# A two-layer hybrid decoder step: the tile scheduler orders VectorE, ScalarE, GpSimd and DMA work with a timeline simulator

## The chip, the core and the metric

The kernel runs on one NeuronCore of one Trainium2 chip. The metric is the device time of one execution in microseconds (us), the median of several. The core's engines work in parallel, each through its own list of instructions from top to bottom: TensorE (PE in the profile, with its weight loads as PEld), VectorE (DVE), ScalarE (ACT), GpSimd (POOL), and SyncE (SP), which here only issues DMA. An instruction that waits for another engine holds up everything behind it in its own list.

## The reference, cut to what is computed

Two layers over 544 tokens (a prompt of 512, and 8 samples of 4), in float32, with a width of 1024:

```python
h = rmsnorm(x, p['norm1_g']) * (1 + mod[:, 1]) + mod[:, 0]
z = h @ p['w_in']          # pooling, retention, short conv, RWKV-7 and the merge gates
yA = pool_mixer(...); yB = retention(...); yC = short conv; yD = rwkv7_mixer(...)
proj = jnp.einsum('btnc,ncd->btnd', branches, p['w_br'])
gates = jax.nn.sigmoid(z[..., COL_GATE:].reshape(B, T, N_BRANCH, D_MODEL))
mixed = jnp.sum(gates * proj, axis=2) @ p['w_out']
x = x + mod[:, 2] * mixed
h2 = rmsnorm(x, p['norm2_g']) * (1 + mod[:, 4]) + mod[:, 3]
up, n_ffn = causal_dwconv(h2 @ p['w_up'], st_ffn, p['ffn_w'])
x = x + mod[:, 5] * ((jax.nn.silu(up[..., :D_FF]) * up[..., D_FF:]) @ p['w_down'])
```

`mod` is a linear map of silu(c), c being the condition of the prompt and of each sample. A last RMSNorm gives y; the new states of all branches are outputs too.

## The kernel before, in words

Activations lie with channels on the 128 partitions and tokens along the free axis, in two halves of 272 tokens (`HS`). Every large product is made in three passes: weights and activations are split into a rounded part (hi) and the rest (lo), and PE adds hi*hi, hi*lo and lo*hi into one PSUM tile (`mm3`, L133 to L135). A **unit** is one block of 128 output channels for one half: 8 blocks of K, so 24 matmuls, or 6 where K is 256. Its result is a `pd` tile. The pool of these (`psd`) has three buffers, so a unit can begin only when the tile three units back, or whichever held its buffer, has been read out.

For the weights `load_unit` issues a DMA into a `raw` tile (three buffers), ACT casts it to `whi` (L113), and DVE subtracts to get `wlo` (L114); `whi` and `wlo` have four buffers each. Activations are split the same way by `split_hilo` (L394 on ACT, L395 on DVE).

The steps of a layer, in PE's order, with the lines the prediction names:

- **Head** (first layer only): `ada_first(k)` makes the modulation of block k (L207 matmuls, L209 copy on ACT, L212 matmuls, L214 and L196 on DVE); L942 on DVE multiplies x by the norm's factor, L290 having made that factor; L297, L300, L301 modulate; `first_units(k)` starts the first six units, k by k.
- **Branches**: the RWKV scan has small matmuls that wait for short copies (L615 on DVE before L620, L481 before L500). `retention` ends with a norm (L388 and L391 on ACT, with loads of the activation table, L872 and L873 on DVE).
- **Gates** (once for each branch): long units whose tile ACT reads out with a sigmoid (L1129), and short `project` units of 6 matmuls, in fours, whose tiles DVE multiplies by the gate (L1111) and which L1113 adds up on GpSimd, or on DVE in the last gates. The last gates also split the sum with L394 and L395.
- **W_out** on that sum: `residual` reads the tile out (L346, and for the second half also L350 and L353), L276 and L279 sum the squares, L287 adds over partitions, L290 inverts, and `norm_half` makes the next input (L309, L297, L394, L395) while the next half's units run.
- **FFN**: units of W_up are read out by ACT (L1274), convolved (L1039 to L1041), and W_down follows, again through `residual`, into the next layer's norm.

Two mechanisms set the order of instructions. On PE it is the order of the code, under `manual_schedule`. On all other engines the scheduler of the tile framework orders the instructions, in the kernel before by its own estimates; a read-out in the code stands under `tc.high_priority()`:

```python
with tc.high_priority():
    V.tensor_tensor(out=a[:, c0:c1] if first else gs, in0=pp[:, :HALF], in1=gs, op=MUL)   # L1111
if not first:
    (V if last else G).tensor_tensor(out=a[:, c0:c1], in0=a[:, c0:c1], in1=gs, op=ADD)    # L1113
if last:
    split_hilo(a[:, c0:c1], mix[m // 4][:, m % 4, c0:c1], mix[2 + m // 4][:, m % 4, c0:c1])
```

## Time and profile before

| | |
|---|---|
| time, median of 3 runs | 1978.6 us (1977.38 to 1979.33) |
| the profiled execution | 1977.9 us, span 1976.1 us |
| PE busy | 1908.5 us, 97% |
| DVE, ACT, POOL busy | 1111.4 us, 831.2 us, 315.7 us |

The profile is that of one execution. Its span runs from the first to the last instruction, so 1.8 us of the execution's own time lie outside it. Busy time counts the instructions themselves. A row of the timeline ends with the idle time before it in square brackets, and with what ended that idle time; idle time on an engine matters only where PE ends up waiting for it.

### The profile page before, as it was taken

Reading aid. Unit: us, or ns where it says so; the run is one execution under the profiler, and the core shown is the slowest. Engines: PE = TensorE matmul, PEld = TensorE weight load, DVE = VectorE, ACT = ScalarE, POOL = GpSimd, SP = SyncE. Lnnn points to the kernel's source line nnn. Section 1 sums busy time; section 2 is a strip of 40 time slices with the busy share of each in tenths; the row PEclk is TensorE's granted clock in tenths of the full one; section 3 lists DMA queues with packets and bytes.
Section 4 is the critical chain, followed back from the end, with each engine's and each line's share of the span. In section 5 each row is a group of like instructions: output and inputs, shape, how many; then the busy total and the mean of one; then the engine's idle time right before and its main releaser. Section 6 shows DMA issues by size and latency. Waiting matters only on the chain.

```text
span 1976.1 us, 39220 instructions
## 1 busy us (share of the span) xinstructions
PE 1908.5 (97%) x16188; PEld 1829.6 (93%) x16188; DVE 1111.4 (56%) x2267; ACT 831.2 (42%) x1581; POOL 315.7 (16%) x627
## 2 busy tenths in 40 slices
PE   5999999999999999999999999999999999999997
PEld 4989888899999998899989899889999999999997
DVE  5466654643565653455673667556335765455565
ACT  4642332452445531435455433326424555243542
POOL 2120123213001210112201201232210012011210
PEclk8999999999999999999999999999999999999998
DMA  7323434423342257622332132124224222222231
GB/s 311 98 87 112 139 117 149 141 82 95 125 148 104 91 205 291 234 86 86 120 130 66 57 106 68 65 95 127 76 85 163 72 80 93 86 86 86 90 101 46
DMA packets 75555, 227.16 MB, mean 115 GB/s; under 512 B 20208, under 2 KB 23072, under 8 KB 73584
## 3 DMA queue, kind: packets, MB, share of 16 engines
q1 hardware_dynamic: 69872, 210.43, 31.9%
q0 software_dynamic: 3536, 11.53, 1.7%
q10 hardware_dynamic: 1968, 2.69, 0.5%
q8 instruction: 127, 2.08, 0.4%
q14 instruction: 52, 0.43, 0.1%
HBM read 213.33 MB, written 9.06 MB: 113 GB/s over the span
## 4 chain that ended last, share of the span: by engine, by line
PE 90%; DVE 5%; ACT 2%; DMA 1%; issue 1%; DVEq 0%; ACTq 0%
PE pd L133 27%; PE pd L135 26%; PE pd L134 26%; PE pm L236 2%; DVE wlo L114 1%; PE pm L673 1%; ACT whi L113 1%; DMA raw<-in_wst 1%; PE pm L500 1%; PE pm L677 1%; PE pm L653 0%; DMA t<-in_wada 0%; PE pm L507 0%; PE pm L620 0%; PE pm L383 0%
## 5 line engine op out<-in xcount | busy, mean ns | idle before, releaser
L133 PE MATMUL pd<-t,whi 128*128 128x272 f32 x4104 | 1207.3, 294 | 7.5 <-DVE zr L350 3.6
L135 PE MATMUL pd<-t,wlo 128*128 128x272 f32 x4104 | 1187.5, 289 | 0.0
L134 PE MATMUL pd<-t,whi 128*128 128x272 f32 x4104 | 1181.8, 288 | 0.1
L133 PEld LDWEIGHTS pd<-t,whi 128*128 128x128 f32 x4104 | 773.9, 189 | 39.9 <-issue 26.4
L134 PEld LDWEIGHTS pd<-t,whi 128*128 128x128 f32 x4104 | 775.7, 189 | 1.3 <-DVE t L395 0.3
L135 PEld LDWEIGHTS pd<-t,wlo 128*128 128x128 f32 x4104 | 774.3, 189 | 0.0
L114 DVE TENSOR_TENSOR wlo<-raw,whi 128x1024 fp32r<-128x1024 f32 x256 | 316.9, 1238 | 301.7 <-ACT whi L113 301.4
L113 ACT CAST whi<-raw 128x1024 fp32r<-128x1024 f32 x258 | 270.5, 1049 | 433.4 <-PE pd L134 419.6
L1276 POOL COPY off<-zr 128x18 f32<-128x18 f32 x88 | 76.2, 866 | 558.8 <-ACT zr L1274 558.8
L346 DVE SCALAR_TENSOR_TENSOR t<-pd,mod,t 128x272 f32<-128x272 f32 (+1 forms) x160 | 76.9, 481 | 112.5 <-PE pd L135 111.6
L1274 ACT COPY zr<-pd 128x272 f32<-128x272 f32 (+2 forms) x264 | 72.7, 311 | 78.4 <-PE pd L135 78.4
L1129 ACT ACTIVATE zr<-pd 128x272 f32<-128x272 f32 x128 | 50.3, 395 | 110.3 <-PE pd L135 106.2
L1111 DVE TENSOR_TENSOR zr<-pd,zr 128x272 f32<-128x272 f32 x96 | 41.1, 437 | 98.8 <-PE pd L135 98.1
L1113 POOL TENSOR_TENSOR t<-t,zr 128x272 f32<-128x272 f32 x64 | 71.3, 1133 | 112.5 <-DVE zr L1111 112.4
L1040 DVE SCALAR_TENSOR_TENSOR zr<-zr,par,zr 128x560 f32<-128x560 f32 x92 | 73.4, 800 | 10.0 <-ACT zr L1039 9.9
L1041 DVE SCALAR_TENSOR_TENSOR zr<-zr,par,zr 128x560 f32<-128x560 f32 x92 | 73.4, 801 | 2.8
L1039 ACT ACTIVATE zr<-zr,par 128x560 f32<-128x560 f32 x92 | 70.2, 765 | 6.8
L394 ACT CAST t<-zr 128x544 fp32r<-128x544 f32 (+1 forms) x96 | 49.5, 530 | 53.4 <-DVE zr L1287 53.0
L395 DVE TENSOR_TENSOR t<-zr,t 128x544 fp32r<-128x544 f32 (+1 forms) x96 | 54.5, 580 | 30.7 <-ACT t L394 30.4
L276 ACT ACTIVATE zr<-t 128x272 f32<-128x272 f32 (+1 forms) x72 | 32.2, 455 | 82.8 <-DVE t L346 54.6
L133 PE MATMUL pd<-t,t 128*128 128x272 f32 x224 | 64.8, 289 | 0.2
L134 PE MATMUL pd<-t,t 128*128 128x272 f32 x224 | 64.5, 288 | 0.0
(283 smaller groups left out, 1770.1 us busy)
## 6 DMA issues: line engine op xcount, KB each, us to landing
raw<-in_wst SPq DMA_DIRECT2D x276, 512.0 KB, 3.4
t<-in_wada SPq DMA_DIRECT2D x32, 1024.0 KB, 9.5
raw<-in_wada SPq DMA_DIRECT2D x24, 512.0 KB, 3.4
zr<-in_rope POOLq DMA_DIRECT2D x16, 272.0 KB, 3.6
t<-in_wada SPq DMA_DIRECT2D x8, 512.0 KB, 6.1
t<-in_xT SPq DMA_DIRECT2D x4, 544.0 KB, 6.1
zr<-zr ACTq DMA_DIRECT2D x32, 68.0 KB, 2.9
t<-in_xT SPq DMA_DIRECT2D x2, 1088.0 KB, 7.1
```

Of the source, the lines that this page charges most:

```text
L113: S.copy(hi, raw)
L114: (G if (l, u) in ((0, 1), (0, 2)) else V).tensor_tensor(out=lo, in0=raw, in1=hi, op=SUB)
L133: PE.matmul(ps, lhsT=a, rhs=xh, start=first, stop=False)
L134: PE.matmul(ps, lhsT=a, rhs=xl, start=False, stop=False)
L135: PE.matmul(ps, lhsT=b, rhs=xh, start=False, stop=last)
L346: V.scalar_tensor_tensor(out=x[:, c0:c0 + npc], in0=ps[:, :npc], scalar=gate[:, m, 0:1], in1=x[:, c0:c0 + npc], op0=MUL, op1=ADD)
L1039: S.activation(cv, u[:, 0:560], AF.Copy, scale=wcol(0))
L1040: V.scalar_tensor_tensor(out=cv, in0=u[:, 1:561], scalar=wcol(1), in1=cv, op0=MUL, op1=ADD)
L1041: V.scalar_tensor_tensor(out=cv, in0=u[:, 2:562], scalar=wcol(2), in1=cv, op0=MUL, op1=ADD)
L1113: (V if last else G).tensor_tensor(out=a[:, c0:c1], in0=a[:, c0:c1], in1=gs, op=ADD)
L1274: pad_evac(lambda o, i, sl: S.copy(o, i), u, ps, half, 2)
L1276: G.tensor_copy(off[:, 22 * s + j], u[:, 512:562].rearrange("p (x t) -> p x t", t=2)[:, 0:25:3, :])
```

## The change

One argument of the tile context. With it the scheduler uses a timeline simulator as its model of the machine when it decides in which order the instructions of DVE, ACT, POOL and the DMA queues stand. PE stays in the order of the code.

```diff
-    with tile.TileContext(nc) as tc:
+    with tile.TileContext(nc, schedule_with_timeline_sim=True) as tc:
         with tc.manual_schedule(engines={mybir.EngineType.PE}):
             tile_hybrid_step(tc, io)
```

The instructions stay the same but for four more loads of the activation table on ACT (two in each layer, between L388 and L391). PE's 14127 rows are the same. Taken as lists, the two DVE orders differ in 1483 lines, those of ACT in 681, of SP in 58 and of POOL in 34. Layer 2 repeats what layer 1 does. Three places in layer 1, all on DVE, follow; names are the program's, with their numbers.

**The last but one gates, their last four short units** (`pd_709` to `pd_712`; L872, L873 and L395 are the end of retention). Before:

```order
L872 TENSOR_TENSOR t4_670_4825<-t4_670_4825,zr_698_5016 128x544
L1111 TENSOR_TENSOR zr_678_4854<-pd_709_5090,zr_678_4854 128x272
L873 TENSOR_TENSOR t4_670_4825<-t4_670_4825,t4_614_4415 128x544
L1111 TENSOR_TENSOR zr_686_4910<-pd_710_5099,zr_686_4910 128x272
L114 TENSOR_TENSOR wlo_715_5129<-raw_713_5126,whi_714_5128 128x1024
L1111 TENSOR_TENSOR zr_696_4989<-pd_711_5108,zr_696_4989 128x272
L1111 TENSOR_TENSOR zr_701_5028<-pd_712_5117,zr_701_5028 128x272
L395 TENSOR_TENSOR t4_653_4663<-t4_670_4825,t4_653_4663 128x544
```

With the change:

```order
L872 TENSOR_TENSOR t4_670_4825<-t4_670_4825,zr_698_5016 128x544
L873 TENSOR_TENSOR t4_670_4825<-t4_670_4825,t4_614_4415 128x544
L395 TENSOR_TENSOR t4_653_4663<-t4_670_4825,t4_653_4663 128x544
L1111 TENSOR_TENSOR zr_678_4854<-pd_709_5090,zr_678_4854 128x272
L114 TENSOR_TENSOR wlo_715_5129<-raw_713_5126,whi_714_5128 128x1024
L1111 TENSOR_TENSOR zr_686_4910<-pd_710_5099,zr_686_4910 128x272
L1111 TENSOR_TENSOR zr_696_4989<-pd_711_5108,zr_696_4989 128x272
L1111 TENSOR_TENSOR zr_701_5028<-pd_712_5117,zr_701_5028 128x272
```

L873 and L395 now stand ahead of the first read-out L1111, and the subtraction of `wlo_715` ahead of the second. On ACT the read-out L1129 of `pd_705` has moved from before the loads of the table for L388 and L391 to behind them, and L394 of the same tile stands ahead of the cast `whi_714`.

**The end of the last gates and the start of W_out** (`pd_841` to `pd_844` are the last four short units; `pd_867` is the first unit of W_out; `zr_829` and `zr_838` are the first token half, which that unit reads, `zr_831` and `zr_840` the second). Before, from the first L395 of these four on:

```order
L395 TENSOR_TENSOR t4_766_5543<-t4_279_2273,t4_764_5541 128x272
L1113 TENSOR_TENSOR t4_279_2273<-t4_279_2273,zr_838_6139 128x272
L1113 TENSOR_TENSOR t4_279_2273<-t4_279_2273,zr_840_6166 128x272
L395 TENSOR_TENSOR t4_766_5543<-t4_279_2273,t4_764_5541 128x272 x2
L114 TENSOR_TENSOR wlo_853_6227<-raw_851_6224,whi_852_6226 128x1024
L346 SCALAR_TENSOR_TENSOR t4_845_6216<-pd_867_6258,mod_4_94,t4_845_6216 128x272
L395 TENSOR_TENSOR t4_766_5543<-t4_279_2273,t4_764_5541 128x272
L114 TENSOR_TENSOR wlo_856_6233<-raw_854_6230,whi_855_6232 128x1024
L114 TENSOR_TENSOR wol_862_6245<-raw_860_6242,woh_861_6244 128x1024
```

With the change, from the subtraction that has moved up furthest:

```order
L114 TENSOR_TENSOR wlo_853_6227<-raw_851_6224,whi_852_6226 128x1024
L1113 TENSOR_TENSOR t4_279_2273<-t4_279_2273,zr_829_6057 128x272
L1111 TENSOR_TENSOR zr_831_6084<-pd_842_6179,zr_831_6084 128x272
L1111 TENSOR_TENSOR zr_838_6139<-pd_843_6190,zr_838_6139 128x272
L1111 TENSOR_TENSOR zr_840_6166<-pd_844_6201,zr_840_6166 128x272
L1113 TENSOR_TENSOR t4_279_2273<-t4_279_2273,zr_831_6084 128x272
L395 TENSOR_TENSOR t4_766_5543<-t4_279_2273,t4_764_5541 128x272
L1113 TENSOR_TENSOR t4_279_2273<-t4_279_2273,zr_838_6139 128x272
L1113 TENSOR_TENSOR t4_279_2273<-t4_279_2273,zr_840_6166 128x272
L114 TENSOR_TENSOR wlo_856_6233<-raw_854_6230,whi_855_6232 128x1024
L114 TENSOR_TENSOR wol_862_6245<-raw_860_6242,woh_861_6244 128x1024
L395 TENSOR_TENSOR t4_766_5543<-t4_279_2273,t4_764_5541 128x272 x2
```

Three weight subtractions (`wlo_853`, `wlo_856`, `wol_862`) that stood behind the pair of L395 now stand ahead of it.

**The second half of W_out while the norm of the first half is made** (`pd_889` and `pd_896` are units of the second half, which L346 and then L350 read out). Before:

```order
L114 TENSOR_TENSOR wlo_912_6699<-raw_910_6696,whi_911_6698 128x1024
L346 SCALAR_TENSOR_TENSOR t4_845_6216<-pd_896_6582,mod_4_94,t4_845_6216 128x240
L395 TENSOR_TENSOR t4_849_6222<-zr_886_6519,t4_847_6220 128x272
L353 TENSOR_TENSOR t4_845_6216<-t4_845_6216,zr_887_6525 128x32
L114 TENSOR_TENSOR wlo_921_6769<-raw_919_6766,whi_920_6768 128x1024
L309 TENSOR_TENSOR zr_890_6537<-t4_845_6216,zr_885_6516 128x272
L309 TENSOR_TENSOR zr_891_6548<-t4_845_6216,zr_885_6516 128x272
L309 TENSOR_TENSOR zr_892_6559<-t4_845_6216,zr_885_6516 128x272
L346 SCALAR_TENSOR_TENSOR t4_845_6216<-pd_905_6635,mod_4_94,t4_845_6216 128x240
L309 TENSOR_TENSOR zr_893_6570<-t4_846_6217,zr_885_6516 128x272
L350 TENSOR_TENSOR zr_894_6576<-pd_889_6530,mod_4_94 128x32
```

With the change:

```order
L114 TENSOR_TENSOR wlo_912_6699<-raw_910_6696,whi_911_6698 128x1024
L353 TENSOR_TENSOR t4_845_6216<-t4_845_6216,zr_887_6525 128x32
L395 TENSOR_TENSOR t4_849_6222<-zr_886_6519,t4_847_6220 128x272
L346 SCALAR_TENSOR_TENSOR t4_845_6216<-pd_896_6582,mod_4_94,t4_845_6216 128x240
L309 TENSOR_TENSOR zr_890_6537<-t4_845_6216,zr_885_6516 128x272
L309 TENSOR_TENSOR zr_891_6548<-t4_845_6216,zr_885_6516 128x272
L309 TENSOR_TENSOR zr_892_6559<-t4_845_6216,zr_885_6516 128x272
L309 TENSOR_TENSOR zr_893_6570<-t4_846_6217,zr_885_6516 128x272
L350 TENSOR_TENSOR zr_894_6576<-pd_889_6530,mod_4_94 128x32
L114 TENSOR_TENSOR wlo_921_6769<-raw_919_6766,whi_920_6768 128x1024
```

L350, the last reader of `pd_889`, now stands ahead of the subtraction `wlo_921` instead of behind it. The same exchange occurs for the units that follow, and at the end of layer 1, where W_down's second half runs beside the norm of layer 2.

Elsewhere: in the head the DVE list has all sixteen L942 ahead of the subtraction `wlo_114` (before, ten of them), and the L214 of block 0 ahead of the last two; ACT has the copies L209 of blocks 0 and 1 ahead of the casts L113 they followed; SP issues the fifth block's condition weights (`in_wada0`) behind seven small loads, and the last three behind three loads of layer weights. In the RWKV scan four of the pooling branch's additions (L1156, L1157, L1172, L1173) stand ahead of the copies that PE's small matmuls wait for.

## Rows read from the trace of the kernel before

**Rows 1.** The page: the span, and busy time by engine.

```profile
span 1976.1 us, 39220 instructions
PE 1908.5 (97%) x16188; PEld 1829.6 (93%) x16188; DVE 1111.4 (56%) x2267; ACT 831.2 (42%) x1581; POOL 315.7 (16%) x627
```

**Rows 2.** Waits of PE: who waits for whom, total us, times, longest.

```profile
PE pm L620 <- DVE gs L615: 10.4, 10, 1.3
PE pm L212 <- ACT t L209: 9.0, 2, 5.5
PE pm L500 <- DVE zr L481: 8.4, 3, 4.0
PE pd L133 <- DVE zr L350: 8.2, 6, 2.8
...
PE pd L133 <- ACT zr L1274: 1.1, 1, 1.1
```

**Rows 3.** The page: groups by line (busy, mean ns, idle before).

```profile
L114 DVE TENSOR_TENSOR wlo<-raw,whi 128x1024 fp32r<-128x1024 f32 x256 | 316.9, 1238 | 301.7 <-ACT whi L113 301.4
```

**Rows 4.** Timeline, last but one gates of layer 1 (start, duration, engine, idle before).

```profile
433.95 0.66 ACT L391 ACTIVATE zr<-zr 128x544 f32<-128x544 f32 x1
...
435.28 0.43 DVE L1111 TENSOR_TENSOR zr<-pd,zr 128x272 f32<-128x272 f32 x1
435.63 0.72 DVE L873 TENSOR_TENSOR t<-t,t 128x544 f32<-128x544 f32 x1
435.77 0.39 PE L133 MATMUL pd<-t,whi 128*128 128x272 f32 x1 [1.25 <-DVE zr L1111]
...
437.15 0.64 ACT L394 CAST t<-t 128x544 fp32r<-128x544 f32 x1
```

**Rows 5.** Timeline, end of the last gates and start of W_out, layer 1.

```profile
535.97 0.44 DVE L1111 TENSOR_TENSOR zr<-pd,zr 128x272 f32<-128x272 f32 x1
...
538.23 1.05 ACT L113 CAST whi<-raw 128x1024 fp32r<-128x1024 f32 x1 [0.27 <-PE pd L134]
...
539.84 0.79 DVE L395 TENSOR_TENSOR t<-t,t 128x272 fp32r<-128x272 f32 x2
...
542.44 1.22 DVE L114 TENSOR_TENSOR wlo<-raw,whi 128x1024 fp32r<-128x1024 f32 x1
543.58 1.22 DVE L114 TENSOR_TENSOR wol<-raw,woh 128x1024 fp32r<-128x1024 f32 x1
```

**Rows 6.** Timeline, second half of W_out, layer 1.

```profile
572.91 1.23 DVE L114 TENSOR_TENSOR wlo<-raw,whi 128x1024 fp32r<-128x1024 f32 x1
...
576.17 0.36 PE L133 MATMUL pd<-t,woh 128*128 128x272 f32 x1 [1.21 <-DVE zr L350]
...
580.53 0.36 PE L133 MATMUL pd<-t,woh 128*128 128x272 f32 x1 [1.10 <-DVE zr L350]
```

**Rows 7.** Timeline, second half of W_down at the end of layer 1.

```profile
1015.17 0.37 PE L133 MATMUL pd<-t,whi 128*128 128x272 f32 x1 [2.82 <-DVE zr L350]
...
1022.59 0.19 DVE L350 TENSOR_TENSOR zr<-pd,mod 128x32 f32<-128x32 f32 x1
...
1023.22 0.29 PE L133 MATMUL pd<-t,t 128*128 128x272 f32 x1
...
1029.63 0.73 PE L287 MATMUL pm<-zr,cst 128*128 128x272 f32 x2 [0.67 <-DVE zr L279]
```

**Rows 8.** Timeline, the head.

```profile
17.70 3.54 DVE L942 TENSOR_TENSOR t<-t,zr 128x272 f32<-128x272 f32 x10
...
20.96 3.61 POOL L114 TENSOR_TENSOR wlo<-raw,whi 128x1024 fp32r<-128x1024 f32 x1 [6.24 <-ACT whi L113]
21.16 1.22 DVE L114 TENSOR_TENSOR wlo<-raw,whi 128x1024 fp32r<-128x1024 f32 x1
...
22.38 2.49 DVE L942 TENSOR_TENSOR t<-t,zr 128x272 f32<-128x272 f32 x1
...
30.85 0.60 PE L133 MATMUL pd<-t,whi 128*128 128x272 f32 x1
```

## The prediction

> **What bounds the kernel now.** The page comes first: PE is busy for 1908.5 of 1976.1 us [rows 1], so all that any order of the other engines can give back is the 67.6 us in which PE stands still. 1908.5 us over 16188 matmuls make 0.118 us for one, 0.7 us for a unit of 6 and 2.8 us for one of 24. PE's list does not change. An instruction that moves on another engine therefore counts only if it moves a moment at which PE is released, and a delay of PE at one place is carried to the end, since all that follows on the other engines depends on PE's results. The view of PE's waits names who releases it late: L212 in the head (9.0 us), the small copies of the RWKV branch (L620 10.4, L500 8.4), and L350 and L1274 as readers of a `pd` tile (8.2 and 1.1) [rows 2]. Third I went through the order place by place: for each read-out of a `pd` tile and each operand of PE that now stands behind something that ran later before, I compared what was put ahead of it with the slack that its reader had. Few places are left over; the others are hidden by the three `pd` buffers or by weights that are ready long ahead. The commonest thing put ahead is a weight subtraction, 1238 ns [rows 3]; DVE waits for its cast for 301.7 us in all, so it is free to be placed in many ways.
>
> **The change, place by place.** Ends below are made from the durations in the rows; DVE instructions in a row overlap a little (ten L942 take 3.54 us, 0.35 each [rows 8]), so a short one counts 0.35.
>
> Last but one gates. Before, `pd_711` waited 1.25 us for the first L1111, which ended at 435.71 [rows 4]. Now L873 and L395 stand ahead of it. L391 ends at 434.3 where it ended at 434.6, since a read-out has left the list ahead of it; L872 and L873, 0.72 each, run to 435.7, L394 (0.64), behind a table load and that read-out, to 436.5, L395 (0.7) to 437.2, L1111 to 437.6: PE starts at 437.6, not 435.8. Of the next unit of 24 the buffer now comes from the second L1111, behind the subtraction of 1.24: 437.6 + 1.2 + 0.4 = 439.2, where PE came to it after two units of 6 (435.8 + 2 x 0.9 with their start) at 437.6. That is +1.6 to +2.0; I take 1.8. Bounds 0.5 (the table load and L391 come earlier than I think) and 3 (L395 slowed by GpSimd). Twice: **+3.6**.
>
> Into W_out. `pd_867` begins when the last short unit ends, about 538.2 (the cast that waited for it began at 538.23 [rows 5]), and needs the L395 of `zr_838` for its 23rd matmul, 22 x 0.125 us later: 540.9. Before, that L395 ended at 540.63 [rows 5], just in time. Now: L1111 ends at 536.4, `wlo_853` at 537.5, eight short ones at 540.3, `wlo_856` and `wol_862` at 542.6 (they overlap to 1.14 each, as 542.44 and 543.58 show), and the two L395 (0.79) at 543.4. PE waits 2.4 us in the middle of a unit. The late L346 of this unit is harmless, since its buffer is wanted three units (8 us) later. Bounds 1.0 and 3.2. Twice: **+4.8**.
>
> Second half of W_out. PE waited 1.21 and 1.10 us for L350, which stood behind the subtraction of 572.91 and, at its next turn, behind five L395 and L279 [rows 6]. Now `wlo_921` and the L395 are behind it: L350 ends at 574.2 where PE's start at 576.17 shows 576.1, and the next at 577.4 where 580.53 shows 580.4, both ahead of PE. But what was passed is late next: the fourth L350 from there has three subtractions ahead of it, and by the same addition ends at 584.85 where PE would arrive at 584.1. So 2.31 gained and some given back: -2.0, bounds -2.3 and 0. Twice: **-4.0**.
>
> Start of W_up: the 1.05 us behind L1274 [rows 2] hang on L1041 of the first convolution pairs, which now stands ahead of an L395 of 0.7 us: **-1.0**, bounds -1.1 and 0; layer 2 had no such wait.
>
> End of layer 1. The same exchange: PE's 2.82 us [rows 7] fall to 0.6, since L350 has two subtractions fewer ahead of it. But of what was passed, three subtractions then stand together ahead of the L350 that releases the last unit of W_down, two of which ran behind it before. With 1.14 for each it is 2.1 later than the 1022.78 at which it ended, so 1024.9, and PE, which began that unit at 1023.22 [rows 7], begins it 1.7 later; the 0.67 us in front of L287 [rows 7] go. Net **+0.7** to +1.0, I take 0.7; bounds -2.8 and +2.5.
>
> Head. The copies L209 of blocks 0 and 1 no longer wait behind a cast, so the 9.0 us at L212 nearly go. That by itself gives nothing: the first units wait for block 0's modulated input, begun before at 30.85 [rows 8]. Now all sixteen L942 and a subtraction stand ahead of it. Two on GpSimd run meanwhile, and beside the first of these one L942 took 2.49 us instead of 0.35 [rows 8]. If both block DVE like that, L942 ends at 17.7 + 16 x 0.35 + 2 x 2.4 = 28.1, then subtraction, L214, L196, two L297 for each of two blocks, L394 (1.2 + 0.4 + 2.2 + 0.6): 32.5, or +1.7. If DVE passes GpSimd by, 4.3 earlier: -2.8. The rows show both: a subtraction on DVE took its usual 1.22 us from 21.16 on, inside GpSimd's 3.61 [rows 8]. I take **+1.5**, nearer to the blocked end, because it is an L942 that was blocked; upper bound +3. [...]
>
> Small things, each a fraction of a 1.24 us subtraction, an L1111 of 0.43 or a pooling addition ahead of a copy: L481 before L500 (+0.3 a layer), an L1113 ahead of an L1111 (+0.25), the pooling additions in the scan less three L620 waits that shorten by an L1111 (+0.4), the last L346 behind the final norm (+0.5 once): **+2.4**, bounds 0 and 6. The four table loads lie where ACT's read-outs have slack of two units, nothing; without that cover 1.3 us each.
>
> Sum: 3.6 + 4.8 - 4.0 - 1.0 + 0.7 + 1.5 + 2.4 = +8.0 us. The profiled execution took 1977.9 us itself, so 1985.9; it lies 0.7 below the median of the runs, so 1986.6 beside that. I forecast **1986**.
>
> **The rivals.** (a) The two places in the gates cost nothing, because the casts, and so the subtractions, come earlier than I place them. For it: raw weights are mostly there long before. Against it: `whi_855` waited for PE until 538.23 [rows 5], so `wlo_856` cannot come early. Without the W_out term: 1985.9 - 4.8 = 1981.1, no change; that is so from the point at which its 2.4 falls under 0.7. (b) GpSimd doesn't block the head: 1985.9 - 4.3 = 1981.6, no change. (c) All L350, L1274 and L212 waits go (18.3 us [rows 2]) and no later L350 pays: 1977.9 - 18.3 + 3.6 + 4.8 + 2.4 = 1970.4, faster; it decides once more than 14.8 of the 18.3 stay. Against it: at both places the passed subtractions meet a later L350. (d) More is lost in the head: ACT now has the first cast of the later layer weights ahead of block 2's L394; if that load lands late, each of block 2 and 3's inputs is late by some 3 us, and small losses reach their upper bound: 1985.9 + 3 + 3.6 = 1992.5.
>
> **How the numbers follow.** A measurement of this kernel can tell about 0.2%, 4 us, from no change. Chances: forecast 0.5; (a) 0.11, (b) 0.11; (c) 0.11; (d) 0.17. So faster 0.11, same 0.22, slower 0.67. The range leaves out most of (c) and a part of (d): 1974 to 1995; the forecast's own is 1982 to 1991.
>
> **What would show it.** In the changed profile: PE waits of about 2 us for L1111 in the last but one gates, and of about 2.4 us for L395 (by then a wait inside a unit) at W_out, in both layers; no L350 wait at the second half's start; L212 gone from the waits and the first unit of the head later than 30.85. I am wrong if the L395 wait isn't there, or if waits that I call gone come back elsewhere on L350.

## The result, and the profile of the changed kernel

The changed kernel takes 1993.6 us (median of four runs, 1989.6 to 1994.7) against 1979.0; the ratio is 1.0069, with a 95% interval of 1.0054 to 1.0084. It is slower by 14.7 us. The forecast was 1986 with a range of 1974 to 1995: the direction held, and the loss is almost twice the +8.0 of the sum. The time lies inside the range, but outside the forecast's own 1982 to 1991.

The page of the changed kernel, to stand beside [rows 1] (the profiled execution is its fastest, 1989.6 us):

```profile
span 1987.8 us, 39277 instructions
PE 1913.2 (96%) x16188; PEld 1833.9 (92%) x16188; DVE 1107.8 (56%) x2267; ACT 834.5 (42%) x1585; POOL 316.6 (16%) x627
```

The span is 11.7 us longer; the other 3 us of the 14.7 are that this execution lies 4.1 below the median of its kernel, and that of [rows 1] 1.1 below its own. The waits, to stand beside [rows 2]:

```profile
PE pm L500 <- DVE zr L481: 9.8, 4, 4.5
PE pm L620 <- DVE gs L615: 9.4, 10, 1.6
PE pd L133 <- ACT t L394: 8.5, 1, 8.5
PE pd L133 <- DVE zr L350: 5.5, 7, 2.2
PE pd L133 <- ACT zr L1129: 4.6, 2, 2.3
PE pd L134 <- DVE t L395: 3.5, 2, 1.8
PE pm L653 <- DVE z L691: 2.4, 2, 1.5
PE pd L133 <- DVE t L1111: 2.1, 3, 0.9
...
PE pm L212 <- ACT t L209: 1.0, 2, 0.5
```

L212 has fallen from 9.0 to 1.0 and L1274 is gone. New are L1129 (twice 2.3), L395 (1.8 and 1.7, with PE's L134 waiting, so in the middle of a unit), L691, and L394 in the head (8.5: the time of the L212 waits, spent at a later line).

Because PE's list is the same in both kernels, the start of each matmul can be set against its start before. The difference (the shift) is a staircase, and each step is what one place costs or gives: waits that grew or went, and also matmuls that run at half speed behind them in one of the two executions (at a granted clock of 0.50 a 128x272 matmul starts 0.227 us behind the one before it, at 1.00 0.125 us). The steps of 0.5 us and more:

| place | forecast, a layer | layer 1 | layer 2 |
|---|---|---|---|
| head, up to 57 us | +1.5 | +2.1 | |
| start of the scan, L500 | in "small" | +1.9 | 0 |
| rest of the scan: PSUM buffers, L653, L620, L742 | in "small" | +1.1 +1.0 +1.2 -0.9 +0.7 -1.2 | +0.7 +1.4 +0.6 -0.8 -0.9 +0.5 |
| matmuls at half speed in the scan, in the execution of before only | | -1.5 | -1.5 |
| last but one gates | +1.8 | +2.7 | +3.2 |
| an L1113 ahead of an L1111 | in "small" | +0.5 | +0.6 |
| into W_out | +2.4 | +2.4 | +3.0 |
| second half of W_out | -2.0 | -2.6 | -2.6 |
| start of W_up | -1.0 | -1.2 | |
| end of layer 1 | +0.7 | +1.9 | |
| end of layer 2 | in "small" | | +0.8 |

In the last but one gates the wait is there, but another releaser than forecast comes first. Timeline of the changed kernel:

```profile
434.90 1.28 ACT L388 ACT_TABLE_LOAD   x1
...
436.71 1.28 ACT L391 ACT_TABLE_LOAD   x1
438.00 0.66 ACT L391 ACTIVATE zr<-zr 128x544 f32<-128x544 f32 x1
438.68 1.28 ACT L1129 ACT_TABLE_LOAD   x1
439.97 0.40 ACT L1129 ACTIVATE zr<-pd 128x272 f32<-128x272 f32 x1
...
440.42 0.39 PE L133 MATMUL pd<-t,whi 128*128 128x272 f32 x1 [2.29 <-ACT zr L1129]
...
441.58 0.43 DVE L1111 TENSOR_TENSOR zr<-pd,zr 128x272 f32<-128x272 f32 x1
...
442.06 0.60 PE L133 MATMUL pd<-t,whi 128*128 128x272 f32 x1 [0.17 <-DVE zr L1111]
```

The L1129 that reads `pd_705` out stands behind three loads of the table of 1.28 us each, and `pd_710` needs the buffer of `pd_705`: PE waits 2.29 for it. When DVE's late L1111 comes to matter, PE is late already, and waits only 0.17 more for it at `pd_711` (0.62 in layer 2). But this L1111 still comes last. It ends at 442.0; less the 4.35 us by which PE was late on arrival that is 437.7, where the text has 437.6, and `pd_711` begins 1.9 us later than before in each layer, for the 1.8 forecast. The rest of the two steps, 0.7 and 1.3, is matmuls at half speed right behind. The granted clock is 0.59 from 440 to 444 us in layer 1, and 0.57 from 1420 to 1424 us in layer 2 (the row is the first of the two; its columns are named further down):

```profile
440.00:444.00 4.00, 3.41 (x14) 3.09 (x15) 2.90 (x6) 2.15 (x4) 1.91 (x2) 0.59 0.00 0
```

At W_out the rows are the forecast, some 7.3 us later (the pair of L395 ends at 550.65 where the text has 543.4): the two subtractions ahead of the pair of L395, and PE inside its unit:

```profile
547.59 1.22 DVE L114 TENSOR_TENSOR wlo<-raw,whi 128x1024 fp32r<-128x1024 f32 x1
548.73 1.22 DVE L114 TENSOR_TENSOR wol<-raw,woh 128x1024 fp32r<-128x1024 f32 x1
549.87 0.78 DVE L395 TENSOR_TENSOR t<-t,t 128x272 fp32r<-128x272 f32 x2
...
550.70 0.39 PE L134 MATMUL pd<-t,whi 128*128 128x272 f32 x1 [1.80 <-DVE t L395]
```

In the second half of W_out L350 stands ahead of the subtraction, the waits of 1.21 and 1.10 [rows 6] are gone, and one of 0.22 comes instead, further on:

```profile
584.03 0.18 DVE L350 TENSOR_TENSOR zr<-pd,mod 128x32 f32<-128x32 f32 x1
584.13 1.21 DVE L114 TENSOR_TENSOR wlo<-raw,whi 128x1024 fp32r<-128x1024 f32 x1
...
594.14 0.36 PE L133 MATMUL pd<-t,t 128*128 128x272 f32 x1 [0.22 <-DVE zr L350]
```

And at the end of layer 1 the wait of 2.82 [rows 7] has become four (0.41, 0.61, 1.72 and 2.18), the last of them behind two subtractions:

```profile
1018.46 0.36 PE L133 MATMUL pd<-t,whi 128*128 128x272 f32 x1 [0.41 <-DVE zr L350]
...
1025.78 0.36 PE L133 MATMUL pd<-t,t 128*128 128x272 f32 x1 [1.72 <-DVE zr L350]
...
1027.83 2.36 DVE L114 TENSOR_TENSOR t<-raw,t 128x1024 fp32r<-128x1024 f32 x2
1030.10 0.19 DVE L350 TENSOR_TENSOR zr<-pd,mod 128x32 f32<-128x32 f32 x1
...
1030.44 0.36 PE L133 MATMUL pd<-t,t 128*128 128x272 f32 x1 [2.18 <-DVE zr L350]
```

### The profile page after: what moved, and what is told of

Its sections match the earlier page's. It is cut to its first block, busy times and chain, and to the rows that moved or that the text cites. A ratio compares the mean times of both kernels' runs of the same rounds, so it can differ in the third digit from the quotient of the medians.

```text
span 1987.8 us, 39277 instructions
## 1 busy us (share of the span) xinstructions
PE 1913.2 (96%) x16188; PEld 1833.9 (92%) x16188; DVE 1107.8 (56%) x2267; ACT 834.5 (42%) x1585; POOL 316.6 (16%) x627
## 4 chain that ended last, share of the span: by engine, by line
PE 84%; DVE 8%; ACT 3%; issue 2%; DMA 2%; SPq 0%; DVEq 0%; ACTq 0%
PE pd L133 26%; PE pd L135 25%; PE pd L134 25%; PE pm L236 2%; DVE wlo L114 1%; PE pm L673 1%; DVE zr L290 1%; DMA raw<-in_wst 1%; PE pm L500 1%; PE pm L653 1%; ACT whi L113 1%; PE pm L507 0%; PE pm L677 0%; DVE t L942 0%; PE pm L620 0%
## 5 line engine op out<-in xcount | busy, mean ns | idle before, releaser
L134 PE MATMUL pd<-t,whi 128*128 128x272 f32 x4104 | 1182.0, 288 | 3.5 <-DVE t L395 3.5
L134 PEld LDWEIGHTS pd<-t,whi 128*128 128x128 f32 x4104 | 775.7, 189 | 5.2 <-DVE t L395 4.1
L113 ACT CAST whi<-raw 128x1024 fp32r<-128x1024 f32 x258 | 270.5, 1049 | 437.6 <-PE pd L134 427.4
L346 DVE SCALAR_TENSOR_TENSOR t<-pd,mod,t 128x272 f32<-128x272 f32 (+1 forms) x160 | 76.3, 479 | 115.9 <-PE pd L135 115.3
L1274 ACT COPY zr<-pd 128x272 f32<-128x272 f32 (+2 forms) x264 | 72.9, 311 | 85.2 <-PE pd L135 85.2
L1111 DVE TENSOR_TENSOR zr<-pd,zr 128x272 f32<-128x272 f32 x96 | 41.0, 436 | 102.7 <-PE pd L135 102.1
L1129 ACT ACTIVATE zr<-pd 128x272 f32<-128x272 f32 x128 | 50.6, 395 | 111.5 <-PE pd L135 103.1
L1113 POOL TENSOR_TENSOR t<-t,zr 128x272 f32<-128x272 f32 x64 | 68.6, 1088 | 121.0 <-DVE zr L1111 120.8
L1040 DVE SCALAR_TENSOR_TENSOR zr<-zr,par,zr 128x560 f32<-128x560 f32 x92 | 73.4, 801 | 7.1 <-ACT zr L1039 7.1
L395 DVE TENSOR_TENSOR t<-zr,t 128x544 fp32r<-128x544 f32 (+1 forms) x96 | 54.2, 578 | 31.8 <-ACT t L394 31.8
L394 ACT CAST t<-zr 128x544 fp32r<-128x544 f32 (+1 forms) x96 | 48.8, 531 | 47.9 <-DVE zr L1287 47.0
```

What stands on the lines that cost most here:

```text
L113: S.copy(hi, raw)
L134: PE.matmul(ps, lhsT=a, rhs=xl, start=False, stop=False)
L346: V.scalar_tensor_tensor(out=x[:, c0:c0 + npc], in0=ps[:, :npc], scalar=gate[:, m, 0:1], in1=x[:, c0:c0 + npc], op0=MUL, op1=ADD)
L1040: V.scalar_tensor_tensor(out=cv, in0=u[:, 1:561], scalar=wcol(1), in1=cv, op0=MUL, op1=ADD)
L1274: pad_evac(lambda o, i, sl: S.copy(o, i), u, ps, half, 2)
```

## The experiments

Most of the kernels are one of the two orders with pieces of the other. The instructions keep their places in the code; a function behind it draws an edge from each instruction of an engine to the next one that a table names, and the table is what an experiment changes:

```python
def pin_order(tc, nc):
    ins = nc.cur_bb.bb.instructions
    for at in ORDER.values():               # one list for VectorE, ScalarE, GpSimd, DMA queue
        for i, j in zip(at, at[1:]):
            tc.add_manual_dep(ins[j], ins[i].name, NoSync, reason="order")
```

Outside the places that an experiment names, the order of each engine's list in its trace is that of the kernel it starts from. Every ratio, and a difference with a sign, is against the kernel before as it ran beside that experiment (medians of 1979.0 to 1980.3).

**The two places in the gates, undone in the changed kernel, and alone in the kernel before.**

```diff
  VectorE, last but one gates (and so in layer 2)
- L872  L873  L395  L1111 pd_709  L114  L1111 pd_710 ...
+ L872  L1111 pd_709  L873  L1111 pd_710  L114 ... L395
  VectorE, end of the last gates
- L114 wlo_853  L1113 ...  L395  ...  L114 wlo_856  L114 wol_862  L395 x2
+ L1113 ...  L395 ... L395 x2  L114 wlo_853 ...  L114 wlo_856  L114 wol_862
  ScalarE, both places: the rows of before
```

> The changed kernel, with the order of before on VectorE and ScalarE at two places of each layer: the last four units of the last but one gates, and the end of the last gates with the start of W_out. Theory (each place counts by its own wait, added up to the end): the traces show +2.7 us and +2.4 us of shift there in each layer, so 1993.6 - 10.2 = 1983.4, and the waits of the first product of pd_710 for L1129 (2.3) and of L134 for L395 (1.8) are gone from the list. Rival 1 (a wait further on swallows what is saved, since something there does not follow PE): above 1988, with another wait longer by the same amount. Rival 2 (the loss is TensorE's clock after waits, not the waits): the waits go and the time falls by clearly more than 10, below 1981, because the matmuls behind the waits are shorter too.

Measured: 1983.7 us, ratio to before 1.0022 (1.0012 to 1.0032). The waits for L395 are gone, and those for L1129 fall from 4.6 to 1.0 us. So 10.0 us come back of the 11.1 that the steps in the table make, and nothing further on swallows much of them. This run and the next change VectorE's and ScalarE's lists together; no run parts the two.

> The kernel before, with the order of the changed kernel on VectorE and ScalarE at those two places of each layer and nowhere else. Theory: 1979.0 + 10.2 = 1989.2, with steps of 2.7 and 2.4 us in PE's start times against before at the two places of each layer. Rival 1: under 1984. Rival 2 (the clock after the waits): over 1991, with PE's busy time up by over 1.5 us. Rival 3 (the two places only hurt because the head or the scan had come late): no step at all, 1979.

Measured: 1994.8 us, 1.0075 (1.0063 to 1.0088). The steps are there (3.1 and 3.7 us in layer 1), so the first theory's places are right, but the whole is +15.4, not +10.2. PE is busy for 1917.5 us, 9.0 more than before: the second rival's sign. Counted from 100 us on, in the stretches with a granted clock of 0.50, the matmuls that follow one another at half speed lose 11.7 us in this execution, against 3.8 in that of before and 4.9 in that of the changed kernel. The largest piece, in the windows (columns: stretch, its length, busy time and count of PE, PEld, DVE, ACT and POOL, the granted clock, the DMA's share and GB/s), first of the kernel before and then of this one, at the second half of W_down in layer 1, where the two have the same order:

```profile
1012.00:1016.00 4.00, 1.18 (x9) 0.99 (x9) 4.00 (x11) 3.70 (x8) 0.00 (x0) 1.00 0.49 156
1016.00:1020.00 4.00, 3.25 (x26) 3.06 (x25) 3.81 (x13) 3.96 (x10) 0.00 (x0) 1.00 0.29 107
1020.00:1024.00 4.00, 4.00 (x33) 3.85 (x32) 3.78 (x11) 4.00 (x8) 0.00 (x0) 1.00 0.42 174
```

```profile
1016.00:1020.00 4.00, 1.60 (x13) 1.38 (x12) 4.00 (x8) 2.49 (x5) 0.00 (x0) 0.96 0.38 118
1020.00:1024.00 4.00, 3.59 (x16) 3.62 (x17) 2.83 (x10) 3.92 (x10) 0.00 (x0) 0.50 0.50 157
1024.00:1028.00 4.00, 3.25 (x15) 2.96 (x15) 2.88 (x10) 1.66 (x3) 0.00 (x0) 0.50 0.00 0
```

In its timeline the wait is the same as in [rows 7]:

```profile
1020.41 0.57 PE L133 MATMUL pd<-t,whi 128*128 128x272 f32 x1 [2.82 <-DVE zr L350]
```

Behind these 2.82 us the kernel before runs on at a granted clock of 1.00, 33 matmuls in 4 us; here the granted clock is 0.50, and 4 us hold 16. 33 matmuls at half speed cost 3.7 us here. Further such stretches, of 12 to 15 matmuls, stand behind the new waits of the gates in both layers and of W_out in layer 2, where before had none: 1.4, 1.7 and 1.7 us.

Such a stretch came without a long wait too. In the scan of the kernel before, PE is busy all the time from 330 to 334 us, 2 us of them with small matmuls (64x8, L704), and then loses 1.6 us in 14 matmuls at half speed; in the changed kernel the same small matmuls, from 337.2 us, are followed by a granted clock of 1.00 (337 to 345 us). The kernel before:

```profile
330.00:334.00 4.00, 4.00 (x95) 3.31 (x94) 2.95 (x6) 1.39 (x3) 3.05 (x4) 1.00 0.29 75
334.00:338.00 4.00, 4.00 (x21) 4.00 (x22) 1.33 (x3) 0.00 (x0) 1.64 (x4) 0.57 0.88 319
```

**The gains alone.** The kernel before, with the changed order only from the second half of W_out to the norm behind it, and at the start of W_up.

```diff
  VectorE, second half of W_out (and so in layer 2)
- L114 wlo_912  L346 pd_896  L395  L353  L114 wlo_921  L309 x3  L346 pd_905  L309  L350 pd_889
+ L114 wlo_912  L353  L395  L346 pd_896  L309 x4  L350 pd_889  L114 wlo_921
```

> The kernel before, with the order of the changed kernel only in the second half of W_out with the norm behind it (both layers) and at the first units of W_up (layer 1). Theory: the waits for L350 go and nothing comes back, -2.6 us in each layer and -1.2 once: 1979.0 - 6.4 = 1972.6. Rival 1 (what was passed is late at the units behind, so half is given back): 1975 to 1977. Rival 2 (the gain needs the late start that the gates made): 1979.

Measured: 1972.6 us (1972.1 to 1973.6), 0.9968 (0.9956 to 0.9980). Its steps are -2.7, -2.6 and -1.2, together -6.5. What was passed costs PE one wait of about 0.2 us in each layer.

**The rest alone.** The changed kernel, with both lists above put back to the order of before.

> The changed kernel with the order of before at all places of the two other lists (the gates, W_out and the first units of W_up), so that what is left of the change is the head, the scan, the end of layer 1 and the short exchanges. Theory by the sum on record: +0.7 (end of layer 1) +1.5 (head) +2.4 (small) = +4.6, so 1983.6. By the steps of the two traces it is 11.7 - 10.2 + 6.4 = +7.9, so 1986.9; then the terms of the head and the small places are too small by 3.3 in all, and the step at the start of the retention's scan (L500) and at two PSUM buffers of the scan shows it. Rival (these differ from execution to execution, since the time of after scattered by 5 us): within 1 us of before, with other steps than in the first trace.

Measured: 1988.3 us, 1.0045 (1.0033 to 1.0057). That is +8.9, so the remaining terms of the sum (4.6) are too small by 4.3. The next four kernels take them apart.

**The head alone, and the head without GpSimd.** The second one is not only an order:

```diff
-        (G if (l, u) in ((0, 1), (0, 2)) else V).tensor_tensor(out=lo, in0=raw, in1=hi, op=SUB)
+        V.tensor_tensor(out=lo, in0=raw, in1=hi, op=SUB)      # in VectorE's list behind the second L301
```

> The kernel before, with the order of the changed kernel only in the head (VectorE, ScalarE and the DMA queue, up to 75 us). Theory (the two GpSimd subtractions hold up L942 on VectorE): the waits at L212 go from 9.0 to about 1 us, two L942 take near 5 us together, the first unit starts about 1.2 us later than before, and the whole is +1.5 to +2.1: 1979.4 + 1.8 = 1981.2. Rival (the head catches up before the units of block 2 and 3, as the L212 waits are gone): within 0.5 of before from 60 us on.

Measured: 1982.4 us, 1.0016 (1.0007 to 1.0025), +3.4. The first unit starts 1.3 later, the shift is 2.2 at 57 us, and a further 1.8 comes at L500, at 118 us, where VectorE's and ScalarE's orders are those of before.

> As the run with the head alone, but the two subtractions of GpSimd in the head stand on VectorE instead, behind the second L301. Theory: without GpSimd beside them each L942 takes 0.35 us, so the sixteen end near 23.8 and not near 28, the first unit starts near 28.5 (32.0 in the changed kernel, 30.85 before), and the total falls by 3 us or so against the run with the head alone. Rival (the long L942 are not due to GpSimd, but to what else the moment holds, the DMA writes or the casts on ScalarE): two L942 still take 2 us or more each, and the first unit comes later by the 2.4 us of the two subtractions.

Measured: 1977.4 us, 0.9989 (0.9980 to 0.9998): 5.0 below the run with the head alone, and below the kernel before. The changed kernel's head first, then this one's:

```profile
18.02 4.95 DVE L942 TENSOR_TENSOR t<-t,zr 128x272 f32<-128x272 f32 x14
...
22.98 4.99 DVE L942 TENSOR_TENSOR t<-t,zr 128x272 f32<-128x272 f32 x2
...
21.60 6.06 POOL L114 TENSOR_TENSOR wlo<-raw,whi 128x1024 fp32r<-128x1024 f32 x2 [6.55 <-ACT whi L113]
...
32.06 0.59 PE L133 MATMUL pd<-t,whi 128*128 128x272 f32 x1 [8.54 <-ACT t L394]
```

```profile
18.04 4.95 DVE L942 TENSOR_TENSOR t<-t,zr 128x272 f32<-128x272 f32 x14
...
22.99 0.78 DVE L942 TENSOR_TENSOR t<-t,zr 128x272 f32<-128x272 f32 x2
...
27.87 0.60 PE L133 MATMUL pd<-t,whi 128*128 128x272 f32 x1 [4.87 <-ACT t L394]
```

Two L942 take 4.99 us beside GpSimd's subtractions and 0.78 without them. The fourteen ahead of them take 0.35 each, although GpSimd's first subtraction is already under way from 21.60. That subtraction, the last 1.38 us of the fourteen beside its start, takes 3.57 us, and the second 2.53.

**The scan alone, and the end of layer 1 alone.** The kernel before, with the changed order from 100 to 429 us and in the same part of layer 2; and from 1004 to 1062 us.

> The kernel before, with the order of the changed kernel only from the branches to the last but one gates (100 to 429 us, and the same part of layer 2). The sum on record has this at about +2.4 in all. Theory from the traces: the copies of the scan's start (L481) are late by 1.4 + 0.5, two units take another PSUM buffer and wait for a later reader (0.8 + 0.8), and L691 comes late (1.1), less 0.9 and a clock that falls elsewhere: +3 to +6, 1982.4 to 1985.4. Rival (the places of the scan are late only because the head is): 1979 to 1980, and no step at these units.

Measured: 1982.5 us, 1.0017 (1.0006 to 1.0028), +3.5. No step at L500 in layer 1: that one came with the head. Steps of 0.8 at `pd_300` (another PSUM buffer than before, waiting 0.8 for an L1111 that reads out `pd_295` in place of `pd_287`), 1.2 and 1.7 at L653 for L691, -0.9 and -0.8 at an L620.

> The kernel before, with the order of the changed kernel only at the end of layer 1 (1004 to 1062 us). Sum on record: +0.7. Theory from the traces: the wait of 2.8 falls to 0.5, two waits of 1.7 and 2.2 come three and four units later, L287 comes sooner: +1.3, and where the clock falls behind these waits up to 1.5 more: 1980.7 to 1982.2. Rival (the order gains as a whole once the first wait is gone): -1 or less.

Measured: 1979.6 us, 1.0004 (0.9995 to 1.0014): +0.65, not told from no change. The steps are -2.3, +1.6, +2.3 and -1.2. The head, the scan and the end of layer 1, each alone, make +7.6 of the +8.9 of the rest; the short exchanges that are left have no run of their own.

**The load of the table at L500.** In the changed kernel the buffer that the first L386 of layer 1 writes was last used by L1001 on GpSimd, and so L386 waits for GpSimd as well as for DVE. In its trace a semaphore instruction of L386 stands on ScalarE's queue at 106.0 us, and the load of the table comes right behind it, at 106.06, after a wait of 2.93. Before, L386 waited for DVE alone; the trace has no such instruction ahead of the first L386 (104.21), and the load came at 101.33, ahead of a wait of 1.59.

```diff
+        if floor is not None and not warmed: S.activation(warm, EPS6, AF.Ln, bias=ZERO); warmed.append(1)
         for c0, c1 in HS:       # the first of these logarithms is L386
```

> The changed kernel with one instruction more: a logarithm of a constant (128x1) on ScalarE ahead of the first L386 of layer 1, so that the load of the table stands ahead of L386's waits. Theory (the first L386 has a second semaphore to wait for, that of GpSimd, and the load of the table stands behind the first of the two waits, 1.28 us on the path of the scan's start): the step at L500 of the scan falls from 1.9 to about 0.6 us, and the total by 1.3, to 1992.3. Rival (L500 is late because of what stands ahead of L481 on VectorE, a subtraction of 1.24 and L1040): the load moves and L500 stays where it is, 1993.6.

Measured: 1991.8 us, 1.0057 (1.0045 to 1.0070). The total alone does not settle 1.3 us; the rows do. ScalarE in the changed kernel and in this one:

```profile
101.34 1.78 ACT L426 ACTIVATE t<-pm,par 128x272 f32<-128x272 f32 x4
106.06 1.28 ACT L386 ACT_TABLE_LOAD   x1 [2.93 <-DVE zr L385]
107.35 1.35 ACT L386 ACTIVATE zr<-zr,eps 128x272 f32<-128x272 f32 x3
```

```profile
101.75 1.79 ACT L426 ACTIVATE t<-pm,par 128x272 f32<-128x272 f32 x4
103.56 1.28 ACT L380 ACT_TABLE_LOAD   x1
104.86 0.29 ACT L380 ACTIVATE warm<-eps 128x1 f32<-128x1 f32 x1
106.51 1.44 ACT L386 ACTIVATE zr<-zr,eps 128x272 f32<-128x272 f32 x3 [1.36 <-DVE zr L385]
```

The load now lies in ScalarE's idle time, and the step at L500 is gone. PE's waits for L481 there, 4.88 us in the changed kernel (0.44 and 4.44), fall to 3.77, against 3.62 in the kernel before: 1.1 of the 1.9 us. The other 0.8 is matmuls of the scan at the lower clock: it stays at 0.50 until 126.7 us in the changed kernel, and is back at 1.00 by 124 in this one and by 123 in the kernel before. The subtraction and L1040 still stand ahead of L481 here, so the rival is out.

**The gates alone, without the wait at the end of layer 1.** The kernel with the gates alone, and the changed order from 1004 to 1024 us with three subtractions moved behind L350 and L346.

```diff
  VectorE, second half of W_down in layer 1, of the changed order
- L114 wlo_1473  ...  L350 pd_1494  L114 ...  L114 x2  L350 pd_1499  L346 pd_1505
+ ...  L350 pd_1494  L114 wlo_1473  L114 ...  L350 pd_1499  L346 pd_1505  L114 x2
```

> The run with the gates alone, and in it the order at the end of layer 1 in which TensorE no longer waits 2.8 us for L350 (nor later in that unit row). In that run's trace the gates' order cost 10.2 us by steps at its own places, and 4.0 us more by matmuls at the lower clock behind the wait of 2.8 us, at 1017 to 1030, where the order is that of before. Theory (the clock falls behind that wait): both go, 1994.8 - 3.0 - 4.0 = 1987.8, and no stretch of slow matmuls there. Rival (the slow stretch comes anyway, wherever the steps of the gates have moved it): 1991.8, with as many slow matmuls near 1017 to 1030 or later.

Measured: 1992.6 us, 1.0068 (1.0053 to 1.0083). The rival held. The wait of 2.82 is gone, but my order brought waits of 1.45, 1.04 and 2.56 for L350 at the units behind it, and behind the last of these, at 1034 to 1040 us, the granted clock is 0.72. So this run does not say what the clock costs when no wait is left there: the edit failed to take the cause away.

**Towards a better kernel.** First all that had gained, with that same order at the end of layer 1:

```diff
  kernel before: order of the second half of W_out and of the start of W_up as above
+ changed head, both GpSimd subtractions on VectorE, early load of the table
+ VectorE, last but one gates: L1111 x3  L872  L1111  L873  L114  L395
+ VectorE, one L620 of the scan, and the end of layer 1 as in the run above
```

> The kernel before with what the runs so far point to: the order of the changed kernel in the second half of W_out and at the start of W_up; its head, with the two subtractions of GpSimd on VectorE and the early load of the table; the order at one L620 of the scan; the first part of its end of layer 1, where L350 and L346 of two units stand ahead of two subtractions; and in the last but one gates the first three L1111 ahead of L872. Theory, place by place: -6.6 (second half, measured), -2.3 (head), -2.5 (1.25 at the gates, twice), -3.0 (end of layer 1), -0.9 (L620) = -15.3, so 1963.8. Rival (what is gained at one place is waited for at the next, or goes into a lower clock): above 1968.

Measured: 1968.6 us, 0.9946 (0.9933 to 0.9960): -11.7. The end of layer 1 lost (2.3 and 0.8 gained; 1.3, 1.2 and 2.5 given back), and in each gate PE now waits 1.2 for an L1129, which the old wait for L1111 had hidden.

> The best kernel so far without its order at the end of layer 1 (there the order of before stands again), and with one exchange on ScalarE in the last but one gates of each layer: the read-out L1129 of the last long unit ahead of a weight cast L113, since TensorE waited 1.22 us for it there. Theory: the end of layer 1 had given back 5.0 us after a gain of 2.0 and 0.75, so -2.3; the gates -1.0 in each layer: 1968.6 - 4.3 = 1964.3. Rival (the waits at the end of layer 1 were worth less than their steps, or the cast that now comes later is waited for at the next unit): 1967 or more, with a new wait for L114 or L113 behind the gates.

```diff
  ScalarE, last but one gates
- L391  L113 whi_714  L1129 pd_707  L394
+ L391  L1129 pd_707  L113 whi_714  L394
  end of layer 1: the order of before
```

Measured: 1966.7 us, 0.9936 (0.9923 to 0.9950), the lowest median of all and 26.9 below the changed kernel. It is 1.9 below the run before it, not 4.3, and since the intervals of the two overlap, neither of its two changes is shown to gain anything. PE still waits 1.03 for L1129 in each gate, one unit sooner, and behind the wait of 2.82 at the end of layer 1, which is back, 12 matmuls at half speed cost 1.4 us in this execution.

## Why the prediction was right, and where its sizes were off

**What bounds the kernel** held: the time moved where PE's release moved, and where its clock did. By the table's steps the sum of +8.0 has become +11.7: gates +2.3 more, W_out +0.6, second half -1.2, W_up -0.2, end of layer 1 +1.2, head +0.6, small things +0.4 (the remainder, with the steps under 0.5). The direction is that of the sum. The waits at the places that it names came out within 0.6 us a term, but for the second half with W_up; what it lacked is a term for the clock, and enough for the small things. That 1993.6 lies in the range is in part luck: it is outside the forecast's own 1982 to 1991, and the range reaches there for the sake of rival (d), which did not occur.

**Last but one gates.** +3.6 forecast, +5.9 by steps, of which 3.9 is the late release of `pd_711` and 2.0 matmuls at half speed. Place, sign and the queue on DVE hold, L1111's end to 0.1 us. The step that failed stands further down in the text: "The four table loads lie where ACT's read-outs have slack of two units, nothing". The units there are short ones of 0.9 us, and the L1129 of `pd_705`, behind L388's, L391's and its own load, is late by more than that: PE waits 2.29 for it. That costs little on top, since L1111 is later still.

**Into W_out.** +4.8 forecast, +5.4 by steps; place, releaser and mechanism are as written, and the subtractions did stand in the way. Rival (a) is out.

**Both gates together** are shown to be the largest loss: undone they give back 10.0 us, alone they cost 15.4. The sum had 8.4 and no term for the clock, which in the run with the gates alone made 7.9 of the loss.

**Second half of W_out and start of W_up.** -5.0 forecast, -6.4 by steps, -6.7 alone. Of the "some given back" little came: PE waits 0.2 us in each layer for an L350 there. This is the half of rival (c) that was true; its other half, that no later L350 pays, failed at the end of layer 1.

**End of layer 1.** +0.7 forecast, +0.65 alone, +1.9 in the changed kernel's trace, where 15 matmuls behind the wait of 2.18 run at half speed (1.7 us; the granted clock is 0.66 from 1030 to 1034 us). The mechanism is the one named, three subtractions together ahead of an L350.

**Head.** +1.5 forecast, +2.1 by 57 us, +3.4 alone. That GpSimd's subtractions hold up L942 is shown (two in 4.99 us beside them, in 0.78 without), and rival (b) is refuted with it. Why the L942 from 21.60 to 22.98 ran at 0.35 beside GpSimd is not shown. Missing was that a changed order also hands out buffers differently: L386 inherits one from GpSimd, and a load of the table comes onto the path at L500, 1.1 us of waiting by the run with the early load. Two slips in the text's addition: the 2.4 that each blocked L942 adds already holds its own 0.35, so 28.1 should be about 27.5 (measured 27.97), and 4.3 less than +1.7 is -2.6, not -2.8 (-3.0 measured without GpSimd). Rival (d) has the nearest number, 1992.5, but its mechanism did not occur: the inputs of blocks 2 and 3 are not 3 us late, the shift stays under 2.7.

**Small things.** +2.4 forecast within bounds of 0 and 6. They make +2.8 with L500, and the scan alone +3.5. But the 2.8 holds a gain that the order did not make: 3.0 us of matmuls at half speed in the scan that stood in the execution of before and not in this one. Without it they are +5.8, at the upper bound: this is the term that the sum had most wrong. Two kinds of place were not on the list, since no row that PE waits for is exchanged there: units that got another PSUM buffer, whose reader is a later one (waits of 0.86 and 0.81 in layer 1), and L691.

**Open** is what decides whether the clock falls. The wait of 2.82 us at the end of layer 1, with the same order in all of them, was followed by a granted clock of 1.00 in the profiled executions of the kernel before and of the second half alone, and by a lower one with the gates alone (0.50 from 1020 to 1028 us), with the head without GpSimd (0.50 from 1016 to 1020), and in the last kernel (0.70 from 1008 to 1012). Each kernel has the profile of one execution, so this may change from one execution to the next; runs of one kernel scatter by up to 8 us. Why the gates cost 5 us more alone than in the changed kernel is therefore placed (slow matmuls, 11.7 against 4.9 us) but not explained.

## What to carry to other kernels

When a scheduler reorders, look for the few places where the engine that bounds the kernel is released, add up the queue ahead of each releaser, and do so on every engine that can release it: here the addition was done for VectorE, and ScalarE's table loads, taken as nothing, made the longest of the new waits in the gates (2.29 us). A change that gains at one kind of place and loses at another can be split, and the halves measured alone: the gains by themselves gave -6.7 us, and with a mended head and gates 13, out of a change that costs 14.7. A long wait that is taken away can uncover a shorter one right behind it (here 1.2 us for L1129 in place of 1.25 for L1111 in each gate), so ask for the next releaser of the same unit before counting the gain.

## What the runs showed of the hardware that was not expected

- TensorE sometimes ran on at half its clock (granted 0.50): 10 to 17 matmuls of 128x272 at about 0.23 us from one to the next, against 0.125 at 1.00, 1.1 to 1.9 us in all, and twice in a row, 3.7, with the gates alone and with the head without GpSimd. That came behind waits of 1.5 to 2.82 us, and in the scan shortly behind 2 us of 64x8 matmuls, without a wait. The wait of 2.82 with the same order around it cost nothing of the kind in the kernel before (granted 1.00 from 1012 to 1028 us), and the same small matmuls nothing in the changed one (1.00 from 337 to 345 us).
- Two 128x272 multiplications on VectorE took 4.99 us beside two subtractions of 128x1024 on GpSimd, and 0.78 without them.
- At the first L386 of layer 1 the load of the activation table (1.28 us) came at 106.06 in the changed kernel, right behind a semaphore instruction at 106.0 and a wait of 2.93, and no longer in the idle time that had hidden it (from 101.33, with no such instruction ahead of it, in the kernel before).
